# Casts of the second weight pinned behind ScalarE's last GELU, and output copies moved to ScalarE, in a fused two-layer MLP

## The chip, the core and the metric

The kernel runs on one core of one Trainium2 chip. The metric is the device time of one execution in microseconds (us), and a kernel's figure is the median over several executions. A change counts as faster or slower from 2% on, but smaller differences can be told apart by the 95% interval of the ratio, which is given with every timed experiment.

## The reference

The computation is a matrix product, a GELU (in its tanh form) and a second matrix product, all in fp32:

```python
# x (8, 1024, 1024), w1 (1024, 4096), w2 (4096, 1024), fp32
h = x @ w1
h = 0.5 * h * (1 + np.tanh(np.sqrt(2 / np.pi) * (h + 0.044715 * h ** 3)))
return (h @ w2).astype(np.float32)
```

## The kernel before

The 8192 rows are taken in eight superblocks of 1024 rows. In superblocks 1 to 7 each layer is done with seven block products in place of eight, so each product needs sums or differences of blocks of the weights and of the activations. In the first layer TensorE does one product as four matmuls of 128x128 by 128x512.

Superblock 0 is different, because it has to get the weights ready while it works. It loads w1 in four *quads* of columns (a raw fp32 tile of 512 KB comes into one of four staging buffers, is cast to 16 bits, and frees the buffer), builds the sums that its first layer needs, and writes the raw 16-bit w1 to memory. Its second layer uses w2 plainly, without block sums, while the sums of w2 are built for later. In superblock 1 the raw w1 is reloaded, its sums are built on VectorE and written to memory, and from superblock 2 on they are loaded ready-made.

These parts matter here. First, the pools, the loading helper and the sums of w1:

```python
up  = tile_pool(bufs=26)   # units: operands of 4 KB per partition     (abridged)
gcp = tile_pool(bufs=4)    # fp32 staging buffers
tp  = tile_pool(bufs=10)   # temporaries (256 KB)
pp  = tile_pool(bufs=8, space=PSUM)

def cast_in(dst, src, cast):
    st = gcp.tile([P] + list(dst.shape[1:]), F32, name="gc")
    load_in_order(st, src)              # loads keep the order of the program
    cast(out=dst, in_=st)

def sum(self, m, sl=slice(None)):       # in MadeQuad, a quad of w1
    make_sum(self.ops, m, self.raw, KH, QW, sl)          # VectorE
    if not self.first:                                   # superblock 1
        nc.gpsimd.dma_start(out=w1_d[self.q][:, m - 1, :], in_=flat(self.ops[m]))
```

Second, one chunk of the first layer. `tt` runs on VectorE and `gelu` on ScalarE. `ahead` starts work on the next quad of w1, in superblock 1 also its sums:

```python
for c in range(NI):
    q, j = divmod(c, QC)
    # ... (ahead(q + 1, 0) if j == 0)
    pb, qb = psum(), psum()
    product(pb, w, 4, True, False)
    v = temp();  nc.scalar.copy(out=v, in_=pb)
    product(qb, w, 5, True, False)
    u = temp();  tt(u, v, qb, SUB)          # before product 3 may add to qb
    # ... (finish of the chunk before: product 6, then GELU "22")
    rb = psum()
    product(rb, w, 1, True, False)
    s = temp();  tt(s, u, rb, ADD)          # before product 7 may add to rb
    product(pb, w, 2, False, True)
    gelu("21", c, pb)
    # ... s2, product 3, GELU "12"
    product(rb, w, 7, False, True)
    # ... c11, GELU "11"
    if j:
        ahead(q + 1, j)                     # sums of the next quad
```

Third, the second layer of superblock 0, in two halves of columns `b`, each with eight PSUM banks:

```python
for q in range(NI // QC):
    # ...
            cast_in(
                raw[f"{a + 1}{b + 1}"][:, j:j + 2, :],
                w2v[b, a, :, c:c + 2, :],
                pool_copy if b == 0 and q < 2 else nc.scalar.copy,
            )
    # ... (matmuls; sums of w2 when b == 1)
for i in range(2 * NQ):                     # the eight banks
    # ... (last matmuls of bank i)
    o = temp()
    if i % 2:
        nc.scalar.copy(out=o, in_=banks[i])
    else:
        nc.vector.tensor_copy(out=o, in_=banks[i])
    last = store(sb, f"{i // NQ + 1}{b + 1}", i % NQ, o)     # GpSimd's queue
```

The order in which an engine's instructions stand in its queue is chosen when the kernel is compiled and may differ from the order of the program, unless something pins it.

## Time and profile before

| | us |
|---|---|
| median of the first three runs (lowest, highest) | 1606.89 (1605.32, 1606.99) |
| span of the profiled run | 1603.7 |
| TensorE idle near the end of superblock 0's first layer, gap A | 7.41 + 0.31 |
| TensorE idle between the halves of its second layer, gap B | 3.34 |
| superblock 1's first matmul | 245.73 |

The first part of the profile page of the kernel before gives busy time, share of the span and number of instructions of each engine:

```profile
PE 1578.2 (98%) x7296; PEld 717.9 (45%) x7296; DVE 819.6 (51%) x1047; ACT 472.3 (29%) x784; POOL 132.1 (8%) x228
```

TensorE (PE) bounds the kernel. The chain of waits of the kernel before shows where it is held up. Its columns are start, length and what ran or was waited for, in order of time:

```profile
106.92 13.66 DMA gc<-in_w_dram
120.60 1.04 ACT u L137
121.65 0.53 ACT g_218 L287
...
129.48 1.02 PE ps L277 x4
130.50 51.38 PE ps L395 x238
...
185.37 4.12 DMA u<-xb
...
190.95 0.70 DVE tmp L443
191.68 54.21 PE ps L395 x244
245.89 96.87 PE ps L277 x448
342.76 96.69 PE ps L461 x448
```

L277 is the first layer, L395 superblock 0's second layer, L461 the second layer of the later superblocks. From 245.89 us on the chain holds nothing but matmuls, so a gain can only come from before. (The chain lets a piece begin where the one before it ended; in the timeline superblock 1's first matmul starts at 245.73. Starts are given by the timeline from here on.) The timeline of TensorE in the kernel before shows the two gaps. A row is start, length, line, operation, output and input, count, and in brackets the idle time just before and what ended it:

```profile
84.77 31.03 PE L277 MATMUL ps<-u 128*128 128x512 f16 x143
123.20 5.97 PE L277 MATMUL ps<-u 128*128 128x512 f16 x20 [7.41 <-ACT g_216 L287]
129.48 1.02 PE L277 MATMUL ps<-u 128*128 128x512 f16 x4 [0.31 <-ACT g_216 L287]
130.34 0.38 PE L395 MATMUL ps<-u,g_215 128*128 128x512 f16 x1
...
191.68 0.59 PE L395 MATMUL ps<-u,g_217 128*128 128x512 f16 x1 [3.34 <-DVE tmp L443]
...
245.73 97.03 PE L277 MATMUL ps<-u 128*128 128x512 f16 x448
342.60 13.98 PE L461 MATMUL ps<-u,g_1959 128*128 128x512 f16 x64
```

Gap A ends with a GELU (L287), so TensorE waited for a PSUM bank. The timeline of ScalarE in the kernel before tells why that GELU was late:

```profile
118.76 1.04 ACT L137 CAST u<-gc 128x1024 f16<-128x1024 f32 x1 [8.00 <-DMA gc<-in_w_dram]
120.60 1.04 ACT L137 CAST u<-gc 128x1024 f16<-128x1024 f32 x1 [0.80 <-DMA gc<-in_w_dram]
121.56 0.62 ACT L287 ACTIVATE g_218<-tmp 128x512 bf16<-128x512 f32 x1
```

Two casts of w2 (L137) stood in the queue ahead of the GELUs, and the first of them waited 8.00 us for its load. After the gap TensorE also ran slowly for a while. The windows of the kernel before give, for each stretch: its length, busy time and count of PE, PEld, DVE, ACT and POOL, the granted TensorE clock (1.00 is full), the busy share of the DMA engines and what they moved in GB/s:

```profile
115.00:120.00 5.00, 0.80 (x4) 0.28 (x3) 0.00 (x0) 1.04 (x1) 0.00 (x0) 0.94 0.93 252
120.00:125.00 5.00, 1.80 (x5) 0.68 (x5) 1.28 (x2) 4.40 (x7) 0.00 (x0) 0.50 0.98 359
```

Gap B is the same pattern on VectorE. In its timeline in the kernel before, the copy of a bank (L443) follows a sum that waits 7.20 us for a transposing load. The last row is taken from the start of superblock 1 and is needed later:

```profile
189.80 1.23 DVE L107 TENSOR_TENSOR u<-u 128x2048 f16<-128x2048 f16 x1 [7.20 <-DMA u<-xb]
190.95 0.68 DVE L443 COPY tmp<-ps 128x512 f32<-128x512 f32 x1
...
245.93 1.23 DVE L107 TENSOR_TENSOR u<-u 128x2048 f16<-128x2048 f16 x1 [0.60 <-PE ps L395]
```

The row at 245.93 is a sum of the third quad of w1 (ten sums, five for each of two quads, come before it). In the program it belongs to chunk 5 of superblock 1; the compiled order put it among chunk 0's work. Here that does no harm: its operands have landed, and its 0.60 us of idle end with TensorE's last matmuls of L395 and not with a load.

### The profile page before, as it was taken

How to read it: one execution, taken by the hardware profiler on the slowest of the kernel's cores; microseconds unless marked ns; L12 is line 12 of the kernel's file. 1: busy time of each engine (PE TensorE's matmuls, PEld its weight loads, DVE VectorE, ACT ScalarE, POOL GpSimd, SP SyncE). 2: the span in 40 equal slices, each digit the busy share in tenths (PEclk: the TensorE clock that was granted, in tenths of full speed). 3: DMA queues.
4: the chain of work that ended last, by engine and by line, in shares of the span. 5: the costliest groups of instructions: out<-in, count | busy, mean ns of one | idle time of the engine just before them, and what ended most of it. 6: DMA issues, size and time to landing. Idle time of an engine off the chain costs nothing.

```text
span 1603.7 us, 18985 instructions
## 1 busy us (share of the span) xinstructions
PE 1578.2 (98%) x7296; PEld 717.9 (45%) x7296; DVE 819.6 (51%) x1047; ACT 472.3 (29%) x784; POOL 132.1 (8%) x228
## 2 busy tenths in 40 slices
PE   7989999999999999999999999999999999999999
PEld 4434444444444444444444444444444444444444
DVE  6855336644455444555445554456534555455433
ACT  4645104431044210441114410244103431044310
POOL 2230113001100012000120000100001000000000
PEclk9999999999999999999999999999999999999999
DMA  9999998674566646546574565746557464544511
GB/s 306 345 316 361 276 397 280 179 288 146 197 188 184 236 171 228 157 153 262 186 221 144 169 238 197 227 131 226 201 203 246 102 265 158 210 157 178 216 53 53
DMA packets 161820, 338.91 MB, mean 211 GB/s; under 512 B 72257, under 2 KB 78401, under 8 KB 160833
## 3 DMA queue, kind: packets, MB, share of 16 engines
q1 hardware_dynamic: 146944, 278.97, 50.4%
q0 software_dynamic: 14784, 58.73, 11.5%
q8 instruction: 57, 0.93, 0.2%
q14 instruction: 35, 0.28, 0.1%
HBM read 266.34 MB, written 85.98 MB: 220 GB/s over the span
## 4 chain that ended last, share of the span: by engine, by line
PE 95%; DMA 3%; DVE 1%; ACT 1%; issue 0%; SPq 0%; POOL 0%; DVEq 0%
PE ps L277 46%; PE ps L461 42%; PE ps L395 7%; DMA gc<-in_w_dram 2%; DVE u L107 1%; ACT u L137 0%; DVE tmp L107 0%; DMA u<-in_x_dram 0%; DMA u<-xb 0%; SPq L115 0%; POOL u L118 0%; ACT g_218 L287 0%; ACT g_216 L287 0%; ACT g_217 L287 0%; ACT tmp L343 0%
## 5 line engine op out<-in xcount | busy, mean ns | idle before, releaser
L277 PE MATMUL ps<-u 128*128 128x512 f16 x3584 | 779.8, 380 | 13.1 <-ACT g_216 L287 7.7
L107 DVE TENSOR_TENSOR tmp<-tmp,ps 128x512 f32<-128x512 f32 x652 | 447.1, 687 | 661.6 <-PE ps L461 333.3
L277 PEld LDWEIGHTS <-u 128*128 128x128 f16 x3584 | 351.1, 98 | 440.3 <-issue 15.9
L461 PE MATMUL ps<-u,gc 128*128 128x512 f16 x2240 | 485.7, 379 | 0.0
L461 PEld LDWEIGHTS <-gc 128*128 128x128 bf16 x2240 | 219.2, 98 | 264.3
L375 POOL DMA_DIRECT2D out_dram<-tmp x112 | 60.6, 542 | 1108.0 <-ACT tmp L481 733.9
L107 DVE TENSOR_TENSOR u<-u 128x2048 f16<-128x2048 f16 (+2 forms) x110 | 123.0, 1152 | 56.6 <-ACT u L137 21.5
L343 ACT COPY tmp<-ps 128x512 f32<-128x512 f32 x128 | 73.0, 570 | 258.2 <-PE ps L277 258.2
L107 DVE TENSOR_TENSOR tmp<-ps,tmp 128x512 f32<-128x512 f32 x128 | 88.4, 691 | 5.9 <-PE ps L277 1.2
L481 ACT COPY tmp<-ps 128x512 f32<-128x512 f32 x28 | 16.4, 586 | 177.3 <-PE ps L461 177.3
L395 PE MATMUL ps<-u,g_217 128*128 128x512 f16 x128 | 49.0, 383 | 3.3 <-DVE tmp L443 3.3
L395 PE MATMUL ps<-u,g_218 128*128 128x512 f16 x128 | 49.0, 383 | 0.0
L395 PE MATMUL ps<-u,g_215 128*128 128x512 f16 x128 | 48.9, 382 | 0.0
L395 PE MATMUL ps<-u,g_216 128*128 128x512 f16 x128 | 48.8, 381 | 0.0
L137 ACT CAST u<-gc 128x1024 f16<-128x1024 f32 x36 | 37.2, 1044 | 37.6 <-DMA gc<-in_w_dram 37.6
L487 ACT COPY tmp<-ps 128x512 f32<-128x512 f32 x28 | 16.4, 586 | 80.3 <-PE ps L461 80.3
L475 ACT COPY tmp<-ps 128x512 f32<-128x512 f32 x28 | 16.4, 586 | 74.9 <-PE ps L461 74.9
L118 POOL CAST u<-gc 128x1024 f16<-128x1024 f32 (+1 forms) x26 | 28.5, 1105 | 73.8 <-DMA gc<-in_w_dram 60.0
L254 POOL DMA_DIRECT2D xb<-in_x_dram x56 | 27.5, 509 | 18.1 <-DMA out_dram<-tmp 14.5
L441 ACT COPY tmp<-ps 128x512 f32<-128x512 f32 x8 | 4.7, 586 | 71.1 <-PE ps L395 71.1
L395 PEld LDWEIGHTS <-g_218 128*128 128x128 bf16 x128 | 12.6, 98 | 18.8 <-issue 3.9
L395 PEld LDWEIGHTS <-g_215 128*128 128x128 bf16 x128 | 12.6, 99 | 15.5 <-issue 0.8
(120 smaller groups left out, 848.8 us busy)
## 6 DMA issues: line engine op xcount, KB each, us to landing
gc<-in_w_dram SPq DMA_DIRECT2D x64, 512.0 KB, 6.8
out_dram<-tmp POOLq DMA_DIRECT2D x112, 256.0 KB, 4.4
u<-w_d_85 SPq DMA_DIRECT2D x49, 512.0 KB, 6.4
u<-w_d_86 SPq DMA_DIRECT2D x49, 512.0 KB, 7.1
u<-w_d_87 SPq DMA_DIRECT2D x49, 512.0 KB, 5.8
u<-w_d_88 SPq DMA_DIRECT2D x49, 512.0 KB, 6.3
u<-w_d_77 SPq DMA_DIRECT2D x42, 512.0 KB, 4.8
u<-w_d_78 SPq DMA_DIRECT2D x42, 512.0 KB, 5.1
```

The costliest lines, as they stand in the source:

```text
L107: nc.vector.tensor_tensor(out=out, in0=in0, in1=in1, op=op)
L118: pool_last[0] = nc.gpsimd.tensor_copy(out=out, in_=in_)
L137: cast(out=dst, in_=st)
L254: nc.gpsimd.dma_start(out=xb[q:q + P, :], in_=x2[s * SB + q:s * SB + q + P, :])
L277: nc.tensor.matmul(bank, lhsT=ops[m][:, k, cs], rhs=xs[m][:, k, :], start=(first and k == 0), stop=(k == KH - 1), skip_group_check=not first,)
L343: nc.scalar.copy(out=v, in_=pb)
L375: return queue.dma_start(out=out2[r0:r0 + P, o0:o0 + OH], in_=src)
L395: nc.tensor.matmul(banks[i], lhsT=g[f"{i // NQ + 1}{a + 1}"][:, c, (i % NQ) * P:(i % NQ + 1) * P], rhs=w[a], start=(c == 0 and a == 0), st ...
L461: nc.tensor.matmul(banks[q], lhsT=a[:, c, :], rhs=pieces[c // QC][:, c % QC, :], start=(first and c == 0), stop=(c == NI - 1), skip_group_ ...
L475: nc.scalar.copy(out=v[q], in_=ps)
L481: nc.scalar.copy(out=c21, in_=ps)
L487: nc.scalar.copy(out=c12, in_=ps)
```

## The change

The intent is to remove both gaps. All of ScalarE's casts of w2 are kept behind the last GELU of superblock 0, so that no GELU can stand behind a cast that waits. `tc.issue_after(x)` keeps the instructions traced inside it behind x in the queue of x's engine. The eight copies of banks that VectorE did go to ScalarE, away from sums that wait for loads.

```diff
+    def act_late_copy(out, in_):
+
+        with tc.issue_after(gelu_last[0].ins):
+            nc.scalar.copy(out=out, in_=in_)
+
+    gelu_last = [None]
 # ...
         def gelu(b, c, src):
-            nc.scalar.activation(out=g[b][:, c, :], in_=src, func=GELU)
+            gelu_last[0] = nc.scalar.activation(out=g[b][:, c, :], in_=src, func=GELU)
 # ...
-                            pool_copy if b == 0 and q < 2 else nc.scalar.copy,
+                            pool_copy if b == 0 and q < 2 else act_late_copy,
 # ...
                 o = temp()
-                if i % 2:
-                    nc.scalar.copy(out=o, in_=banks[i])
-                else:
-                    nc.vector.tensor_copy(out=o, in_=banks[i])
+                nc.scalar.copy(out=o, in_=banks[i])
                 last = store(sb, f"{i // NQ + 1}{b + 1}", i % NQ, o)
```

## The prediction

> **What bounds it.** TensorE: busy 1578 of 1603.7 us, 95% of the chain of waits; from 245.9 us on that chain is only matmuls. A gain can only come from TensorE's gaps before. After the start-up the timeline shows two.
> - Gap A, 115.8 to 123.2 us (7.4 us), at the end of superblock 0's first matmul. ScalarE's queue has casts of w2 between its GELUs: after 110.8 it stands 8.0 us before a cast whose load has not landed, while GELUs that free PSUM banks wait behind it. Then seven matmuls run at 0.43 us pitch instead of 0.216 (granted clock 0.50: 1.5 us), and 0.3 us follows. Together 9.2 us. (The Trainium skill, "TensorE: Matmul & The Clock Gate", Part 1, gives half clock after an idle window; this trace agrees.)
> - Gap B, 188.3 to 191.7 us (3.3 us, plus about 0.8 us at half clock): a bank's copy on VectorE stands behind a sum that waits 7.2 us for a transposing load of x.
>
> **What the change does.** 24 casts of 1.04 us (12 of them ahead of the last GELU now) all go behind it; A's wait cannot occur, and second-layer matmuls begin near 121 us instead of 130.3. The first two quads are cast on GpSimd by 103.6: 27 us of work for TensorE. Eight copies move from VectorE (0.69 us) to ScalarE (0.59 us); banks finish every 1.3 us, so ScalarE keeps up and B goes. Upper bound of the gain: 9.2 + 4.1 = 13.3 us, which would give 1593.5.
>
> **What it costs.** Four staging buffers hold uncast w2 tiles until about 122.5, so loads stop there. Before, the eighth ScalarE cast ends near 127; my estimate after, four casts then a round trip of about 6 us, is 133: the load chain runs about 6 us late. It cannot catch up: from 120 to 240 us the DMA engines mostly move 360 to 420 GB/s (windows), near the 435 that the skill's "Perfetto Trace Analysis" (Roofline) gives for the 16 engines; the trace agrees. Estimated consequences:
> 1. The last four casts end near 177 instead of 170.7, while half 0's banks finish from 167. Its copies queue behind them; the second half needs bank 0 at 176.3. New gap of 1 to 3 us.
> 2. Superblock 1 would start near 235. Its kept w1 lands in time (213.4 before, 220 after). But the output stores on GpSimd's queue went out only at 243.6, behind two copies waiting for reloaded w1. Ten temporaries: eight hold outputs, so superblock 1's third waits for a store. If that order stays, stores leave at 246 to 250, TensorE stops after five products (near 239.5), and the gain is lost, or slightly more. If the compiled order puts stores first, some 7 to 11 us remain.
>
> Weighed equally: about 6 us.
>
> **Prediction: 1601 us, range 1592 to 1611.** Faster by over 2%: 0.01; within 2%: 0.975; slower by over 2%: 0.015.
>
> **Right if** gap A is gone, ScalarE runs GELUs unbroken to about 122 and casts after it, w2's casts end 5 to 7 us later, no copy of a bank is on VectorE in superblock 0, and superblock 1's first matmul starts at 231 to 237. **Step 2 wrong** if TensorE has no gap between 235 and 255. **Lag wrong** if casts end before 173.
>
> **What would make it wrong.** The compiled order of casts, copies and stores: another store order decides between 1594 and 1610. A lag over 10 us would make it slower than before.

## The result, and the profile after

| | before | after |
|---|---|---|
| median of four runs on the same chip (lowest, highest), us | 1606.11 (1602.64, 1606.99) | 1608.7 (1607.54, 1609.84) |
| profiled span, us | 1603.7 | 1608.0 |
| superblock 0's second layer begins, us | 130.34 | 122.02 |
| superblock 1's first matmul, us | 245.73 | 234.24 |
| superblock 1's second layer begins, us | 342.60 | 347.18 |

The ratio of the times is 1.002, with a 95% interval of 1.0002 to 1.0038: the same within 2%, and if anything a little slower. A ratio here is the mean time of one kernel's runs over that of the other's in the same rounds, so it is not quite the ratio of the medians.

The table tells the story. At superblock 1's first matmul the changed kernel was 245.73 - 234.24 = 11.49 us ahead. At the end of that superblock's first layer it was 4.6 us behind. So about 16.1 us were given back within about 113 us of work that the change does not touch. The first part of the profile page of the kernel after:

```profile
PE 1581.0 (98%) x7296; PEld 718.5 (45%) x7296; DVE 814.6 (51%) x1039; ACT 478.3 (30%) x792; POOL 132.5 (8%) x228
```

VectorE and ScalarE exchanged eight instructions, as intended. TensorE's busy time rose by 2.8 us, for as many matmuls. The timeline of TensorE in the kernel after (L284 is the first layer, L402 superblock 0's second; columns as before):

```profile
122.02 57.57 PE L402 MATMUL ps<-u,g 128*128 128x512 f16 x266
179.89 0.59 PE L402 MATMUL ps<-u,g 128*128 128x512 f16 x2 [0.30 <-ACT tmp L447]
181.53 52.88 PE L402 MATMUL ps<-u,g 128*128 128x512 f16 x244 [1.04 <-ACT tmp L447]
234.24 3.62 PE L284 MATMUL ps<-u 128*128 128x512 f16 x16
240.41 1.02 PE L284 MATMUL ps<-u 128*128 128x512 f16 x4 [2.55 <-DVE tmp L107]
248.04 31.84 PE L284 MATMUL ps<-u 128*128 128x512 f16 x136 [6.61 <-DVE tmp L107]
282.05 1.02 PE L284 MATMUL ps<-u 128*128 128x512 f16 x4 [2.17 <-DVE tmp L107]
283.25 64.10 PE L284 MATMUL ps<-u 128*128 128x512 f16 x288 [0.17 <-DVE tmp L107]
347.18 13.98 PE L465 MATMUL ps<-u,g 128*128 128x512 f16 x64
```

Gaps A and B are gone; 0.30 + 1.04 us are left between the halves. But superblock 1, which had no gap before, now stops after four products, after five, and again near 280 us: 2.55 + 6.61 + 2.17 us, and 0.17 us more at 283.25, 11.5 us together. The matmuls after the long gap ran at half clock: eleven of them took 4.6 us at 248.04 to 252.65 and eight more 3.3 us from 283.25, at twice the 0.216 us that a matmul takes at full clock, so 3.8 us more. That accounts for about 15.3 of the 16.1 us.

The gaps end with VectorE. Its timeline in the kernel after:

```profile
236.26 3.50 DVE L107 TENSOR_TENSOR u<-u 128x2048 f16<-128x2048 f16 x3 [1.34 <-DMA u<-raw_d]
239.68 0.68 DVE L107 TENSOR_TENSOR tmp<-tmp,ps 128x512 f32<-128x512 f32 x1
246.17 1.23 DVE L107 TENSOR_TENSOR u<-u 128x2048 f16<-128x2048 f16 x1 [5.81 <-DMA u<-raw_d]
247.31 1.46 DVE L107 TENSOR_TENSOR tmp<-tmp,ps 128x512 f32<-128x512 f32 x2
...
279.58 1.23 DVE L107 TENSOR_TENSOR u<-u 128x2048 f16<-128x2048 f16 x1 [4.39 <-DMA u<-raw_d]
```

The rows with `u<-u` are sums of w1, those with `tmp<-tmp,ps` are superblock 1's own work on its banks. Chunk 0's subtraction at 239.68 stood behind three sums. Its addition at 247.31, which frees the bank for product 7, stood behind the third quad's sum, which waited 5.81 us for its reload from `raw_d`. It is the same sum that stood harmlessly at 245.93 before. The order hardly changed here; what changed is that superblock 1 began 11.49 us sooner, while the reloads came later. The chain of waits of the kernel after agrees:

```profile
269.55 9.93 DMA u<-raw_d
...
283.25 64.10 PE ps L284 x288
347.34 96.69 PE ps L465 x448
```

The reloads were late because the loads of w2 were. ScalarE's timeline in the kernel after shows GELUs to the end of the layer and four casts at once behind them:

```profile
122.95 0.63 ACT L294 ACTIVATE g<-tmp 128x512 bf16<-128x512 f32 x1 [0.24 <-DVE tmp L107]
123.48 3.87 ACT L137 CAST u<-gc 128x1024 f16<-128x1024 f32 x4
```

Until 123.5 us the four staging buffers were full of uncast tiles. The windows of the kernel after show that the DMA engines then moved nothing for 5 us, and that 120 us later, with TensorE stopped, they were full:

```profile
115.00:120.00 5.00, 5.00 (x25) 2.23 (x23) 2.75 (x4) 2.15 (x5) 0.00 (x0) 1.00 0.84 183
120.00:125.00 5.00, 5.00 (x25) 2.25 (x23) 3.20 (x4) 3.51 (x6) 0.00 (x0) 1.00 0.00 0
...
245.00:250.00 5.00, 1.96 (x5) 0.71 (x5) 2.57 (x4) 0.00 (x0) 1.61 (x3) 0.50 1.03 419
```

The lag of the loading chain against the kernel before was 8 to 9 us at the casts of the first half's last quad of w2 and the second half's first, 12.5 us at the last cast (it ended at 183.25 in place of 170.7) and 10 us at the first sum of the reloaded w1 (223.5 in place of 213.4).

One link more lies between this lag and the sum at 246.17. The second of the two reloads that it adds was issued only at 238.65 us (231.89 before) and landed at 246.07. Its issue had itself waited 7.2 us for a sum on VectorE (in the kernel before, 3.7 us for a matmul), presumably until one of the 26 units came free. If so, a late sum of one quad also makes the reload of the next quad late. The waits of SyncE's queue in the kernel after, from 230 to 245 us (what for, us in total, times, longest):

```profile
SPq L159 <- DVE u L107: 11.5, 3, 7.2
```

### The profile page after: what moved, and what is told of

It is laid out like the page before. It is cut to its first block, busy times and chain, and to the rows that moved or that the text cites. A ratio compares the mean times of both kernels' runs of the same rounds, so it can differ in the third digit from the quotient of the medians. Undisturbed runs are those within 1.5% of the kernel's fastest.

```text
span 1608.0 us, 18980 instructions
## 1 busy us (share of the span) xinstructions
PE 1581.0 (98%) x7296; PEld 718.5 (45%) x7296; DVE 814.6 (51%) x1039; ACT 478.3 (30%) x792; POOL 132.5 (8%) x228
## 4 chain that ended last, share of the span: by engine, by line
PE 83%; DMA 1%; DVE 0%; issue 0%; DVEq 0%
PE ps L465 42%; PE ps L284 41%; DMA u<-raw_d 1%; DVE tmp L107 0%; DVE u L107 0%; DVEq L107 0%
## 5 line engine op out<-in xcount | busy, mean ns | idle before, releaser
L284 PE MATMUL ps<-u 128*128 128x512 f16 x3584 | 784.0, 381 | 17.1 <-DVE tmp L107 13.1
L284 PEld LDWEIGHTS <-u 128*128 128x128 f16 x3584 | 351.8, 98 | 447.9 <-issue 26.2
L294 ACT ACTIVATE g<-tmp 128x512 bf16<-128x512 f32 x256 | 161.1, 630 | 296.6 <-DVE tmp L107 296.6
L465 PE MATMUL ps<-u,g 128*128 128x512 f16 x896 | 195.7, 379 | 0.0
L107 DVE TENSOR_TENSOR gc<-g,g 128x2048 bf16<-128x2048 bf16 x140 | 169.0, 1219 | 27.4 <-PE ps L465 27.4
L294 ACT ACTIVATE g<-ps 128x512 bf16<-128x512 f32 x256 | 152.2, 596 | 99.0 <-PE ps L284 98.7
L350 ACT COPY tmp<-ps 128x512 f32<-128x512 f32 x128 | 73.0, 570 | 259.3 <-PE ps L284 259.3
L465 PEld LDWEIGHTS <-g 128*128 128x128 bf16 x896 | 87.7, 98 | 105.7
L402 PE MATMUL ps<-u,g 128*128 128x512 f16 x512 | 111.0, 379 | 1.3 <-ACT tmp L447 1.3
L402 PEld LDWEIGHTS <-g 128*128 128x128 bf16 x512 | 50.1, 98 | 62.1 <-issue 2.1
L485 ACT COPY tmp<-ps 128x512 f32<-128x512 f32 x28 | 16.4, 587 | 177.3 <-PE ps L465 177.3
L491 ACT COPY tmp<-ps 128x512 f32<-128x512 f32 x28 | 16.4, 586 | 80.3 <-PE ps L465 80.3
L479 ACT COPY tmp<-ps 128x512 f32<-128x512 f32 x28 | 16.4, 586 | 74.9 <-PE ps L465 74.9
L137 ACT CAST u<-gc 128x1024 f16<-128x1024 f32 x24 | 24.8, 1044 | 25.2 <-DMA gc<-in_w_dram 25.1
```

Of the source, the lines that this page charges most:

```text
L107: nc.vector.tensor_tensor(out=out, in0=in0, in1=in1, op=op)
L137: nc.scalar.copy(out=out, in_=in_)
L284: nc.tensor.matmul(bank, lhsT=ops[m][:, k, cs], rhs=xs[m][:, k, :], start=(first and k == 0), stop=(k == KH - 1), skip_group_check=not first,)
L294: gelu_last[0] = nc.scalar.activation(out=g[b][:, c, :], in_=src, func=GELU)
L402: nc.tensor.matmul(banks[i], lhsT=g[f"{i // NQ + 1}{a + 1}"][:, c, (i % NQ) * P:(i % NQ + 1) * P], rhs=w[a], start=(c == 0 and a == 0), st ...
L465: nc.tensor.matmul(banks[q], lhsT=a[:, c, :], rhs=pieces[c // QC][:, c % QC, :], start=(first and c == 0), stop=(c == NI - 1), skip_group_ ...
```

## The experiments

The theories, with the letters under which some expectations name them:

- **L**, the main one: the loads run late, and in VectorE's queue sums of w1 that wait for reloads stand ahead of superblock 1's own work.
- **T**, as the prediction's second consequence had it: superblock 1 lacks temporaries, because they hold superblock 0's outputs until the stores have landed.
- **C**: the additional copies on ScalarE cost the time.
- **W**: it is the lateness itself, the weights that come 10 us late, and no order of a queue.

Twelve kernels ran in three batches. Those of one batch ran on the same chip and share the runs of the kernel before, whose medians were 1605.95, 1606.45 and 1606.01 us (11 runs each). All gave correct results. In the diffs "-" is the kernel after unless said otherwise.

### e1_pin_only: the pin without the moved copies

```diff
-                nc.scalar.copy(out=o, in_=banks[i])
+                if i % 2:
+                    nc.scalar.copy(out=o, in_=banks[i])
+                else:
+                    nc.vector.tensor_copy(out=o, in_=banks[i])
```

> Only the first half of the change: w2's casts go behind the last GELU; the outputs are copied alternately on VectorE and ScalarE as before. Theory L (the pin makes the load chain about 9 to 12 us late, and what waits for that chain on an in-order engine stops TensorE): gap A is gone, but the copy of bank 6 of the first half stands on VectorE behind the sum of x that now gets its transposed blocks near 199 instead of 189.5 us; TensorE stops near 179 until about 201, superblock 1 starts near 255 and then has no gap. About 1616 us, 0.5 to 0.7% slower than before. Theory C (the loss comes from the ScalarE copies, which delay the casts of the second half): faster than before by 8 to 10 us, about 1598.

Measured: 1610.91 us, ratio 1.0028 (1.0016 to 1.004). It is not faster than the kernel after, against what C expected: without the copies on ScalarE nothing is gained. (The last kernels below, which keep these copies and are the fastest, leave C nothing.) The size was expected higher, because gap B was expected to come back and did not. This time the compiled order put that bank's copy ahead of the waiting sum. Superblock 1 had gaps of 0.63, 5.82, 2.30 and 4.70 us. The timeline of VectorE in this kernel shows both a wait for a store and one for a reload:

```profile
247.90 0.69 DVE L107 TENSOR_TENSOR tmp<-tmp,ps 128x512 f32<-128x512 f32 x1 [3.48 <-DMA out_dram<-tmp]
...
282.21 1.23 DVE L107 TENSOR_TENSOR u<-u 128x2048 f16<-128x2048 f16 x1 [6.92 <-DMA u<-raw_d]
```

### e2_copies_only: the moved copies without the pin

```diff
-                            pool_copy if b == 0 and q < 2 else act_late_copy,
+                            pool_copy if b == 0 and q < 2 else nc.scalar.copy,
```

> Only the second half of the change: ScalarE copies all plain outputs; casts of w2 stay where they were. Both theory L and theory T (below, temporaries and stores) expect gap A as before, gap B gone, superblock 1 to start about 4 us earlier (242 us) and at most a gap of 1 us there, since the loads are not late: about 1602.5 us, 0.2 to 0.3% faster than before. Theory C: slower than before, 1608 or more.

Measured: 1607.78 us, ratio 1.0009 (0.9997 to 1.002), 5 us above what was expected. Gap B was gone, so the moved copies do remove it. But gap A came out at 9.28 us in place of 7.41 us: ScalarE stood 8.78 and then 1.90 us before casts in this run. And a new gap of 2.85 us opened at 251.76, where a temporary waited for a store that had not landed. Even this small gain in time made superblock 1 meet something that was not ready.

### e4_sums_behind: the sums of w1 behind superblock 1's own work

On VectorE, the sums of a later quad stay behind the last operation of their chunk.

```diff
-            for m in ((), (4,), (1, 3), (7, 6))[step]:
-                quads[q].sum(m)
+            with ExitStack() as pinned:
+                if sb == 1 and q and step:
+                    pinned.enter_context(tc.issue_after(own[0].ins))
+                for m in ((), (4,), (1, 3), (7, 6))[step]:
+                    quads[q].sum(m)
 # ...
-            tt(c11, u, rb, ADD)
+            own[0] = tt(c11, u, rb, ADD)      # tt returns the instruction
```

> The changed kernel, with superblock 1's sums of w1 for later groups of four columns put behind the VectorE work of the chunk in which they are written, so that a sum waiting for a late reload no longer stands before TensorE's own evictions. Theory L with VectorE's order as the place of the wait: the gaps of 2.6, 6.6 and 2.2 us at 238, 241 and 280 us and their slow matmuls (together about 16 us) go; superblock 1 starts at 234 and runs through: 1592 to 1595 us, 0.8% faster than before. Theory T (the prediction's: temporaries held by late stores stop superblock 1): the gaps stay, 1607 to 1611. Theory W (the weights themselves come too late, whatever the order): the gap moves to weight loads at about 258 us, 1600 or more.

Measured: 1602.78 us, ratio 0.9982 (0.997 to 0.9995). It is 6 us better than the kernel after, but about 8 us or more short of what L expected. No sum was waited for any more; in place of three gaps in superblock 1 there was one, 5.99 us before 244.65. The timeline of VectorE in this kernel names another cause:

```profile
243.91 1.46 DVE L107 TENSOR_TENSOR tmp<-tmp,ps 128x512 f32<-128x512 f32 x2 [7.06 <-DMA out_dram<-tmp]
```

This is the wait that T foresaw, and L alone is not the whole cause. The store that was waited for had been issued at 230.11 and landed 13.68 us later.

### e7_temps: one more temporary

```diff
-    tp = ctx.enter_context(tc.tile_pool(name="tp", bufs=10))
+    tp = ctx.enter_context(tc.tile_pool(name="tp", bufs=11))
```

> The changed kernel with eleven temporaries of 256 KB instead of ten, nothing else. Theory T (superblock 1's third temporary waits for a store): the store is one later in the ring, the gap at 238 to 248 us shrinks by several us, 1604 or less. Theory L: the gap ends when the reload of w1 lands, so no change, 1607 to 1610 us, within 0.1% of the changed kernel.

Measured: 1606.9 us, ratio 1.0007 (0.9995 to 1.0019). Gaps of 6.04 and 3.74 us remained, both behind sums that waited for reloads (5.24 and 5.96 us). T alone is not the cause either.

### e3_pool_half: no lateness in the first half

The casts of the first half of w2 all go to GpSimd, which has time for them, so the staging buffers come free early.

```diff
-                            pool_copy if b == 0 and q < 2 else act_late_copy,
+                            pool_copy if b == 0 else act_late_copy,
```

> The changed kernel, but all casts of the first output half's w2 are on GpSimd (sixteen instead of eight), so that only the second half's casts are pinned on ScalarE and the loads need not stop between 115 and 123 us; VectorE's order stays as it was before the change (36 sums ahead of superblock 1's first subtraction). Theory L (the late load chain is the cause): w2's last cast ends 1 to 4 us later than before the change instead of 12.5 us; the small gap at 180 us goes; superblock 1 starts at about 233 and has one gap of 4 to 7 us, since it starts 12 us sooner than the reloads were laid out for. 1599 to 1603 us, 0.2 to 0.4% faster than before. If lateness is not the cause: as the changed kernel, 1607 to 1610.

Measured: 1606.71 us, ratio 0.9999 (0.9987 to 1.0011), against 1599 to 1603 us expected by L. The lateness was mostly cured: the last cast ended at 173.6 us, and no sum stopped TensorE. But one gap of 12.03 us, where 4 to 7 us were expected, stood before 249.30. The timeline of VectorE in this kernel:

```profile
248.56 1.47 DVE L107 TENSOR_TENSOR tmp<-tmp,ps 128x512 f32<-128x512 f32 x2 [13.10 <-DMA out_dram<-tmp]
```

The stores were issued only at 239.0 to 249.0, behind writes of w1's sums on GpSimd's queue, and TensorE stopped after exactly five products. This is the wait of the prediction's second consequence, but it comes first only where no sum stops TensorE before it: here because the loads are not late, in e4 because the sums stand behind. In the kernel after the sums stop TensorE first.

### e9_stores_act: e4, with the stores on another queue

```diff
-        queue = nc.gpsimd if sb < NSB - 1 else nc.sync
+        queue = nc.scalar if sb == 0 else nc.gpsimd if sb < NSB - 1 else nc.sync
```

On top of e4. The next superblock's cast of x is tied to a write of w1 in place of the last store, which is no longer on its queue; this holds for the next two kernels too.

> Both walls taken away in the changed kernel: superblock 1's later sums of w1 behind the VectorE work of their chunk, and superblock 0's stores on ScalarE's queue. The load chain stays as late as in the changed kernel. Two-walls theory: superblock 1 starts at 234 us and has no gap over 1 us; 1592 to 1596 us, 0.7 to 0.8% faster than before. If the weights themselves are late (theory W): a gap near 258 us and 1598 or more.

Measured: 1601.32 us, ratio 0.9964 (0.9952 to 0.9976), 5 us or more above what was expected. The stores went out from 224.4 us on, but landed 8.4 to 16.1 us later, 12.4 us in the median (9.0 in e4), and gaps of 1.61, 0.36 and 5.25 us remained, from waits for stores. The Trainium skill ("DMA: Bandwidth & Descriptors", section "Issuing engines are not separate DMA queues") says that transfers started by different engines run on the same 16 DMA engines and interleave. This trace agrees: another queue let the stores start sooner, and they then took longer.

### e11_after_stores_act: the kernel after, with the stores on another queue

The same change of the queue without the pinned sums.

> The changed kernel with superblock 0's output stores issued from ScalarE's queue instead of GpSimd's, where they stand behind the writes of w1's sums (the next cast of x is tied to one of those writes in exchange). Nothing else. The last kernels suggest two walls that end at nearly the same time: VectorE's sums that wait for reloaded w1, and temporaries that wait for stores. Theory L alone: VectorE's sums are still in front, the gaps at 238 to 248 us shrink by at most 2 us: 1605 to 1609. Theory T alone: they go: 1600 or less.

Measured: 1609.93 us, ratio 1.0016 (1.0004 to 1.0028). The gaps were 1.16, 5.23 and 6.25 us, and a sum waited up to 8.46 us for a reload. To send the stores early does nothing while the sums hold VectorE.

### e10_all: e9, with the first half's casts on GpSimd

> As the run before, and the first half's w2 all cast on GpSimd. The load chain is early again and the gap of about 1.3 us at 180 us goes as well: 1591 to 1595 us, not slower than the run before; the candidate for a version that beats both.

Measured: 1603.22 us, ratio 0.9983 (0.9971 to 0.9995). It was expected to be no slower than e9; it came out 1.9 us slower, which the intervals do not settle. In superblock 1 one gap of 5.68 us, behind a wait for a store, and two under 1 us remained. The gap between the halves did not go either (0.56 + 0.94 us), though the last cast ended at 170.5 us: now ScalarE's copies of banks waited for stores, up to 2.37 us. So lateness cured, sums out of the way and stores issued early are not enough: the stores also have to land early.

### e14_writes_behind: the writes of w1's sums behind the stores

This gives the stores the way by order, not by another queue. The writes of w1's sums stay behind superblock 0's last store on GpSimd's queue, so that they cannot fill the DMA engines ahead of the stores.

```diff
-                nc.gpsimd.dma_start(out=w1_d[self.q][:, m - 1, :], in_=flat(self.ops[m]))
+                with tc.issue_after(stored[0].ins):      # superblock 0's last store
+                    nc.gpsimd.dma_start(out=w1_d[self.q][:, m - 1, :], in_=flat(self.ops[m]))
 # ... the same in copy_plain
```

> The changed kernel with the second of these edges alone: the writes of w1's sums behind superblock 0's last store; VectorE's sums stay in front. Theory L: VectorE still waits for reloaded w1, but the reloads have the DMA engines more to themselves and land sooner, so the gaps at 238 to 248 us (2.6 and 6.6 us) shrink to 3 to 6 us in all and the one at 280 us shrinks as well: 1599 to 1604 us. Theory T alone: all gaps go, 1596 or less.

Measured: 1599.45 us, ratio 0.9959 (0.9941 to 0.9976), but with a spread from 1597.84 to 1607.71 that no other kernel had. The profiled run was the slowest one: gaps of 3.57 and 6.66 us, a sum waiting 6.71 us for a reload, no wait for a store. What tells its quick runs from its slow ones stays open, since only one was profiled. The median says that in most of them this order alone brought back a good part of the gain.

### e13_both_behind: both orders

e4 and e14 together: the sums behind superblock 1's own work, the writes behind the stores. The casts of w2 are as late as in the kernel after.

> The changed kernel with two edges for superblock 1: its later sums of w1 stand behind the VectorE work of their chunk, and its writes of w1's sums to memory stand behind superblock 0's last output store on GpSimd's queue. So neither a late reload nor a store that stands behind 7 MB of writes should stop TensorE, though the load chain is as late as in the changed kernel. Two-walls theory: superblock 1 starts at 234 us and runs through with no gap over 1 us; 1592 to 1596 us, 0.7 to 0.8% faster than before. If the DMA engines as a whole are the limit there (they move 420 GB/s), whatever the order: a gap of some 5 us stays and 1600 or more.

Measured: 1592.12 us (1591.13 to 1592.8), ratio 0.991 (0.9896 to 0.9924). The stores landed after 4.1 to 8.1 us, 5.4 in the median (10.7 in the kernel after). Superblock 1 runs through; the timeline of TensorE in this kernel:

```profile
180.17 52.88 PE L410 MATMUL ps<-u,g 128*128 128x512 f16 x244 [1.03 <-ACT tmp L455]
232.89 96.86 PE L288 MATMUL ps<-u 128*128 128x512 f16 x448
```

The last cast still ended at 181.6 us, 11 us later than in the kernel before. So W falls: the lateness costs 1 us between the halves and nothing else. A limit of the DMA engines as a whole falls too. From 200 to 255 us they moved 367 GB/s in this kernel, 374 before and 395 after.

### e15_all_behind: e13, with the first half's casts on GpSimd

> As the first of these, and the first half's w2 all cast on GpSimd, so that the loads do not stop at 115 to 123 us. The 1.3 us at 180 us go too: 1591 to 1595 us, equal to the first or 1 to 2 us faster.

Measured: 1591.8 us, ratio 0.9909 (0.9895 to 0.9924), which is e13's within its spread. The gap at 180 us is gone as well, and from 85 us on TensorE has no gap. e13 and e15 are the best versions found; both beat both kernels by about 0.9% to 1%.

### e17_before_both_behind: the control

The two orders of e13 on the kernel *before*, without the change.

> Control: the kernel before the change with the same two edges. It has no gap in superblock 1 to lose, and keeps gaps A and B: within 0.15% of before, 1604 to 1608 us. If it is faster by 5 us or more, the gain of the other kernels is not the change's gain set free but something the edges do by themselves.

Measured: 1605.98 us, ratio 0.9998 (0.9984 to 1.0011). The timeline of TensorE in this kernel:

```profile
123.47 6.00 PE L288 MATMUL ps<-u 128*128 128x512 f16 x20 [7.81 <-ACT g L298]
...
191.22 54.51 PE L410 MATMUL ps<-u,g 128*128 128x512 f16 x244 [2.61 <-DVE tmp L458]
245.57 96.86 PE L288 MATMUL ps<-u 128*128 128x512 f16 x448
```

Without the change the two orders are worth nothing, since superblock 1 starts late enough at 245.57 us. With them, the change is worth 1605.98 - 1592.12 = 13.9 us. Without them it is worth nothing. Neither is enough alone.

## Why the prediction was right or wrong

The measured 1608.7 us lies inside the range of 1592 to 1611 us, and "within 2%" was right. But the middle, 1601 us, was 7.7 us too low, and the sign of the small difference was wrong: a gain of about 6 us was predicted and none came.

- **Gaps A and B go: right.** GELUs ran unbroken to the last one at 122.95 us, the second layer began at 122.02 us (predicted near 121), and no copy of a bank was left on VectorE in superblock 0. The prediction counted 13.3 us in both; 11.49 us had been won at superblock 1's start and 1.34 us was lost between the halves, together 12.8 us. The upper bound of the gain, a time of 1593.5 us, is what e13 reaches once superblock 1 is ready for it (1592.12 us).
- **The lag of the loads: right direction, too small.** It was estimated as about 6 us ("four casts then a round trip"), with the last casts near 177 us. It measured 8 to 9 us at first, 12.5 us at the last cast, 10 us at the reload of w1. At the end the casts alternate with copies of banks in one queue. This term was mis-sized, but e13 shows that its size alone costs almost nothing. ("A lag over 10 us would make it slower than before" came true in the kernel after; e13, as late and faster than before, shows that the lag alone is not why.)
- **Consequence 1, a new gap of 1 to 3 us between the halves: right**, 1.34 us.
- **Superblock 1 starts at 231 to 237 us: right**, 234.24 us.
- **Consequence 2 is the step that failed.** It said of the kept w1 that it "lands in time (213.4 before, 220 after)". The first quad's raw blocks came at 223.5 us, still in time; those of the third quad did not, and its sum stood in VectorE's in-order queue ahead of chunk 0's addition. That row was to be seen in the trace of the kernel before, at 245.93 us. It did no harm there, and so it was not looked at. From this the alternative failed: "If the compiled order puts stores first, some 7 to 11 us remain." The compiled order did let stores out sooner, the first at 232.4 in place of 243.6 us, and nothing remained.
- **What the runs showed in its place: two walls at nearly the same time.** One is the sums waiting for reloads (5.81 and 4.39 us), the other the temporaries waiting for stores. Take away the first alone, and the second costs 5.99 us (e4). Cure the lateness alone, and the second costs 12.03 us (e3). Take away the second alone, and the first remains in e14's profiled run, its slowest; how much of it remained in the quicker ones is not known. Take away both, and the whole gain appears (e13), though the loads are as late as ever.
- **"Step 2 wrong if TensorE has no gap between 235 and 255"** did not apply: gaps were there, 2.55 and 6.61 us, but not for the reason given. The sign chosen could not tell the two causes apart; the releaser in brackets on VectorE could. That the time lies inside the range is therefore partly luck: its upper part stood for stores that stop superblock 1, and the sums, which the prediction did not have, stopped it for about as long.

The Trainium skill ("PSUM — Partial Sum Buffer", section "Engine vs sequencer instructions") says that the queues of ScalarE, VectorE and GpSimdE are strict FIFO. The traces agree for the two engines at which it was looked at: ScalarE stood 8.00 us before a cast with GELUs behind it, VectorE 5.81 us before a sum with an addition behind it. The prediction used this for the gap that the change removes, and did not ask it of the superblock that the change moves forward.

Not settled: the spread of e14, and why the compiled order put e1's bank copy ahead of the sum and the kernel before's behind it.

## What to carry to other kernels

When a change makes a stage begin sooner, go through everything that stage takes first (operands still loading, buffers still held by stores, instructions that stand ahead in each in-order queue) and ask of each whether it is ready at the new time; slack that cannot be seen in the old trace is where the gain goes. When one wait is taken away and the gain does not come, look for a second wait just behind it before giving up the theory, and test both together, with a control that has both cures but not the change. Pin the order of what waits for memory behind what TensorE waits for, on every engine, since the compiled order of one queue can change when another part of the program does.

## What the Trainium skill lacked or had wrong

- "DMA: Bandwidth & Descriptors", section "Anatomy of one DMA": it gives a fixed part of about 2 us and a part by size, but no figure for a transfer that starts behind a backlog. In the kernel after, a store of 256 KB landed in 2.0 us (median) in the quiet last superblock, where SyncE's queue issues it, and in 2.3 us at the quickest from GpSimd's queue. Superblock 0's last stores took 5.4 us (median) with the writes behind them (e13), 10.7 us in the kernel after and up to 16.1 us in e9, from ScalarE's queue. A buffer's return can therefore not be planned from the size alone.
- "TensorE: Matmul & The Clock Gate", Part 1: it gives half clock after an idle window of about 3.4 us. What it says of short idle times that come often gives no length. A single gap need not be so long here. In the kernel after, a gap of 2.17 us, four matmuls at full speed and 0.17 us of idle were followed by eight matmuls at twice the usual time (granted clock 0.52 from 283.2 to 286.6 us), while after 2.55 us at 240.41 the four matmuls that followed were at full speed.
- No page has the pattern of a wait that stands ahead in an in-order queue and appears only when the stage behind it starts sooner: the same sum stood idle 0.60 us before, for TensorE, and 5.81 us after, for its reload.
